# An encoder trunk on one core: two-pass partition sums, an early last norm, a ring of its own for the operand sums, constants loaded by the mix

## The chip, the cores and the metric

The kernel runs on one core of one Trainium2 chip. The core has engines that each run their own instructions strictly in order: TensorE (PE, matmuls, with the weight loads shown as PEld), VectorE (DVE), ScalarE (ACT) and GpSimd (POOL); SyncE (SP) issues most DMA transfers, GpSimd some. The metric is the device time of one execution in microseconds (us). In the names of the trace `out<-in` stands for what an instruction writes and reads, with buffer numbers left out.

## The reference

Two layers (DEPTH 2) work on x of 512 tokens by 1024 channels. Each layer is a feed-forward block, a token-mixing block of three branches, and a second feed-forward block; a last norm ends the program. Cut to what matters here:

```python
def rmsnorm(x, g):
    y = x * lax.rsqrt(jnp.mean(x * x, axis=-1, keepdims=True) + NORM_EPS)
    return y * g

def swiglu_ffn(h, w_in, w_out):            # w_in 1024 x 5632, w_out 2816 x 1024
    gate, up = jnp.split(h @ w_in, 2, axis=-1)
    return (jax.nn.silu(gate) * up) @ w_out

# in rwkv7_mixer (8 heads of 64), and in gla_mixer (4 heads of 128):
kk = kk / jnp.maximum(jnp.linalg.norm(kk, axis=-1, keepdims=True), 1e-12)
bonus = jnp.sum(r_h * k_h * r_k, axis=-1, keepdims=True) * v_h
o = o * lax.rsqrt(jnp.mean(o * o, axis=-1, keepdims=True) + NORM_EPS) * norm_w

for l in range(DEPTH):
    x = x + 0.5 * swiglu_ffn(rmsnorm(x, ffn1_norm[l]), ffn1_w_in[l], ffn1_w_out[l])
    h = rmsnorm(x, mix_norm[l])
    ...                                    # RWKV-7, gated linear attention (GLA), memory attention
    x = x + merged @ w_out[l]
    x = x + 0.5 * swiglu_ffn(rmsnorm(x, ffn2_norm[l]), ffn2_w_in[l], ffn2_w_out[l])
return rmsnorm(x, final_norm)
```

All data are float32.

## The kernel before

**Layout.** Activations lie transposed: channels on the 128 partitions, the 512 tokens along the row. x is eight tiles of 128x512. A sum over channels or over the 64 or 128 channels of a head is therefore a sum over partitions, and is made on TensorE: a matmul with a constant matrix of ones (`ones`), of ones in blocks of 64 (`blk`) or with a column of ones (`one`). These constants and some masks lie side by side in one array `cst` in memory.

**Split products.** A large product runs as three matmuls of type fp32r: each operand is split into `hi`, a rounded copy that ACT writes, and `lo`, the remainder that DVE writes by subtracting `hi`. The products are hi*hi, lo*hi and hi*lo. Plain fp32 matmuls are used where the operands are not split, among them the partition sums.

**A feed-forward block** (`ffn`, L787) goes over 11 column blocks twice (b = 0, 1), and after each eleven it multiplies by the second matrix, eight output tiles. A column block is done in one of two ways. `whole` (L800) multiplies 256 columns directly, with four weight tiles `wraw` of 128x512 (256 KB each) and 48 matmuls of 512 tokens. The other way (`loads` L815, `begin` L829, `middle` L840, `end` L850) is a scheme with seven smaller products instead of eight. It works on two halves of the tokens with sums of operands, and takes 84 matmuls of 256 tokens. It needs sums of activations, made once per block by `half_sums` (L739), and sums of weights. The weight sums are begun by the transfers themselves: `fs`, a tile of 128x2x512, is first filled from SP's queue with one 256 KB weight part written twice, and then GpSimd issues a second transfer into it that adds two other parts (`accum_op=ALU.add`). `wa` is one more part on its own. The first `NWHOLE` = 2 (L28) column blocks with b = 0 are whole, so that the sums can be made meanwhile; all others are done in the second way.

**Rings.** A tile name's tag has a fixed number of buffers. A new use waits until the oldest user's readers are through. `fs` has three buffers, and in the kernel before the tile in which `half_sums` makes its differences (`t`, L748) uses the same tag, so the four of these and the first weight sums of each feed-forward block go through one ring of three.

**The norm of a block** (`norm_in` L685, `rstd` L719): ACT squares the eight x tiles, DVE adds them up to `sqa`, four small fp32 matmuls with `one` sum over partitions into `ps_f`, ACT takes the root (`rt`, after an ACT_TABLE_LOAD), DVE the reciprocal, four fp32 matmuls with the identity (`ps_f<-cst,rt`) broadcast it, and DVE copies it to `rs`. The column blocks need `rs` only after their products. The last norm (`finish`, L1596) uses the same function after the last product and then scales the eight x tiles and stores them.

**Order.** The program is not issued as it is written. A Recorder notes every operation; a planner (`cost` L323, `choose` L385) then sets one order for each engine and for SP from estimated durations, and `issue` (L541) writes it out. It also decides when a transfer is issued; it gives a transfer a duration of its own, with no account of others in flight. All instructions are written in one helper, so every row of the trace shows line L288, and tile names tell them apart.

Of the kernel before, what the change touches and what calls it, by code (L numbers as in the profile page):

```python
# [19 lines left out]
P = 128  # L20
# [7 lines left out]
NWHOLE = 2  # L28
# [18 lines left out]
for _name, _w in (("ident", 128), ("blk", 128), ("mrwkv", 128),  # L47
                  ("eye", 64), ("in4", 64), ("up1", 128), ("up2", 128), ("lev4", 128),
                  ("lev8", 128), ("lev16", 128), ("reset", 512), ("mgla", 256), ("ones", 128)):
    CONST[_name] = (_n, _w)  # L50
    _n += _w
# [504 lines left out]
class Net:  # L556
# [14 lines left out]
    def c(self, name):  # L571
        o, w = CONST[name]
        return self.cst[:, o:o + w]
# [15 lines left out]
    def setup(self):  # L589
# [10 lines left out]
        self.cst = self.const.tile([P, NCONST - 384], F32, name="cst", tag="cst")  # L600
        for c0, c1 in ((0, P), (P, NCONST - 384)):
            nc.sync.dma_start(out=self.cst[:, c0:c1], in_=I["cst"][:, c0:c1])
# [6 lines left out]
        nc.vector.memset(self.one, 1.0)  # L609
        self.yd = self.dram.tile([3, P, T], F32, name="yd", tag="yd")  # L610
# [15 lines left out]
    def mix_params(self):  # L626
        nc, I, l = self.nc, self.I, self.l
        c = self.gp.tile([P, 384], F32, name="mgla", tag="mgla")
        nc.sync.dma_start(out=c, in_=I["cst"][:, NCONST - 384:])
        self.mgla = c[:, 0:256]  # L630
        self.ones = c[:, 256:]
# [44 lines left out]
    def split(self, hi, lo, src, scale=None):  # L676
# [4 lines left out]
        else:  # L681
            nc.scalar.activation(hi, src, AF.Copy, scale=scale)
            nc.vector.scalar_tensor_tensor(lo, src, scale, hi.bitcast(F32), ALU.mult, ALU.subtract)

# [54 lines left out]
    def half_sums(self, pool, xs, norm):  # L739
# [6 lines left out]
        for q in range(4):  # L746
            h = pool.tile([P, 4, H], F32, name="fh", tag="fq", bufs=2)
            t = pool.tile([P, 4, H], F32, name="fs", tag="fs", bufs=3)  # L748
# [38 lines left out]
    def ffn(self, w_in, w_out, norm, aside=None):  # L787


        nc = self.nc  # L790
        with ExitStack() as ctx:
# [4 lines left out]
            for b in range(2):  # L796
# [66 lines left out]
                if b == 0:  # L863
                    for j in range(NWHOLE):
# [8 lines left out]
                if aside is not None and b == 0:  # L873
                    aside(pool)
                for o in range(KD):
# [93 lines left out]
    def rwkv_gates(self, hp, hf, wz, r, k, v):  # L969
# [4 lines left out]
        if hf == 0:  # L974
# [3 lines left out]
            sq, self.nrm_k = (self.lr.tile([P, T], F32, name=n, tag="ush", bufs=2) for n in ("ksq", "knrm"))  # L978
            nc.scalar.activation(sq, self.kk, AF.Square)
            psn = self.small("i")  # L980
            nc.tensor.matmul(psn, self.c("blk"), sq, start=True, stop=True)
# [23 lines left out]
    def rwkv_first(self, hp, hf, r, k, v, kk, kh, a, G):  # L1005
# [96 lines left out]
        nc.tensor.matmul(ps, self.c("blk"), rk, start=True, stop=True)  # L1102
# [290 lines left out]
    def gla_pair(self, pool, hp, al, yh, yl, between):  # L1393
# [70 lines left out]
        for j in range(2):  # L1464
# [14 lines left out]
            nc.tensor.matmul(ps, self.ones, sq, start=True, stop=True)  # L1479
# [116 lines left out]
    def finish(self, out):  # L1596
        nc = self.nc
        rs, _ = self.rstd(self.x, T, D, self.pool("fin", 1), copy=False)
        for k in range(KD):
            nc.vector.scalar_tensor_tensor(self.x[k], self.x[k], self.pcol("final_norm", k), rs, ALU.mult, ALU.mult)  # L1600
# [79 lines left out]
```

## Time and profile before

| what | value |
|---|---|
| time, median of 3 runs | 2659.07 us (2658.54 to 2660.87) |
| the profiled execution | 2659.52 us, of which the span of instructions is 2657.5 us |
| mean granted TensorE clock | 0.996 |

The program's stretches, with PE's busy time in each and the mean busy share of the 16 DMA engines:

| stretch, us from the span's start | what | PE busy us | DMA share |
|---|---|---|---|
| 0 to 60 | start of the first feed-forward block | 50.68 of 60 | 0.84 |
| 60 to 367 | rest of it | 307.00 of 307 | 0.59 |
| 367 to 975 | mix of layer 0 | 603.77 of 608 | 0.25 |
| 975 to 1332 | second feed-forward block | 356.36 of 357 | 0.58 |
| 1332 to 1690 | first feed-forward block of layer 1 | 355.86 of 358 | 0.60 |
| 1690 to 2300 | mix of layer 1 | 606.50 of 610 | 0.26 |
| 2300 to 2640 | second feed-forward block | 337.49 of 340 | 0.56 |
| 2640 to 2657 | last norm and stores | 3.94 of 17 | 0.33 |

A row of the timeline has the start, the duration, the engine, the operation and how many of it follow each other; in brackets stands how long the engine was idle before, and what it waited for. Matmuls overlap in these rows, so their rate is read from start to start. A row of the waits has the engine's tile that waited, what released it, the idle time, the number of waits, and the longest. SPq and POOLq are the issues of transfers by these engines; a DMA row has the time from issue to landing. In a table of windows the columns are the stretch; its length and PE's busy time (and instructions); the busy time of PEld, DVE, ACT and POOL; the granted clock; the DMA share; and the rate in GB/s.

### The profile page before, as it was taken

What the parts mean: (1) busy time and instruction counts of PE and PEld (TensorE: products, weight loads), DVE (VectorE), ACT (ScalarE), POOL (GpSimd) and SP (SyncE); (2) the same over time, 40 slices, a digit from 0 to 9 for tenths busy, and PEclk for the clock granted to TensorE, in tenths of its full rate; (3) what the DMA queues carried; (4) which work ended last, traced back from release to release, by engine and by line L of the source; (5) the groups of instructions that cost most, each with busy time, mean ns of one, the idle gap of its engine ahead of it and who ended that gap; (6) DMA issues with size and microseconds to landing.
All of it is one profiled execution on the core that took longest, in us unless ns stands there. A gap on an engine that the chain in (4) does not pass through costs nothing.

```text
span 2657.5 us, 43379 instructions
## 1 busy us (share of the span) xinstructions
PE 2621.6 (99%) x16136; PEld 2299.9 (87%) x16136; DVE 1909.5 (72%) x3915; ACT 1403.3 (53%) x2727; POOL 91.9 (3%) x194
## 2 busy tenths in 40 slices
PE   8999999999999999999999999999999999999997
PEld 7989988888888889899899898878888888898996
DVE  8949666687886569678497594766888864794873
ACT  7626457465554356446465363665655543663552
POOL 0000000000000001000000000000000000010000
PEclk9999999999999999999999999999999999999998
DMA  8837342211121348565386463422212123584642
GB/s 233 205 107 181 117 147 80 103 62 62 64 66 66 108 137 203 139 153 125 108 203 159 128 159 123 152 85 83 70 58 80 60 80 100 159 201 120 170 110 79
DMA packets 127859, 321.98 MB, mean 121 GB/s; under 512 B 13312, under 2 KB 28096, under 8 KB 127648
## 3 DMA queue, kind: packets, MB, share of 16 engines
q1 hardware_dynamic: 116128, 277.26, 34.2%
q0 software_dynamic: 11520, 41.95, 8.9%
q8 instruction: 127, 2.08, 0.3%
q14 instruction: 84, 0.69, 0.1%
HBM read 307.10 MB, written 12.06 MB: 120 GB/s over the span
## 4 chain that ended last, share of the span: by engine, by line
PE 88%; DVE 7%; DMA 3%; ACT 1%; issue 1%; SPq 0%; DVEq 0%; POOL 0%; ACTq 0%; POOLq 0%
PE ps_b L288 56%; PE ps_i L288 16%; PE ps_f L288 7%; PE ps_c L288 7%; PE ps_y L288 2%; DMA fs<-in_ffn_in_dram 2%; DVE wlo L288 1%; DVE lo L288 1%; DVE t L288 0%; DMA wraw<-in_ffn_in_dram 0%; DVE sqa L288 0%; DVE x L288 0%; DVE Z L288 0%; DVE fs L288 0%; DVE knrm L288 0%
## 5 line engine op out<-in xcount | busy, mean ns | idle before, releaser
L288 ACT ACTIVATE whi<-wraw 128x512 fp32r<-128x512 f32 x522 | 320.9, 616 | 580.7 <-PE ps_b L288 527.0
L288 DVE TENSOR_TENSOR wlo<-wraw,whi 128x512 fp32r<-128x512 f32 (+1 forms) x520 | 347.7, 669 | 332.9 <-ACT whi L288 326.5
L288 PE MATMUL ps_b<-xhi,whi 128*128 128x512 f32 (+1 forms) x880 | 354.1, 403 | 0.1
L288 PE MATMUL ps_b<-xlo,whi 128*128 128x512 f32 (+1 forms) x880 | 351.8, 400 | 0.0
L288 PE MATMUL ps_b<-xhi,wlo 128*128 128x512 f32 x864 | 347.0, 402 | 0.0
L288 PE MATMUL ps_b<-mhi,wlo 128*128 128x512 f32 x704 | 277.2, 394 | 0.0
L288 PE MATMUL ps_b<-mlo,whi 128*128 128x512 f32 x704 | 275.8, 392 | 0.0
L288 PE MATMUL ps_b<-mhi,whi 128*128 128x512 f32 x704 | 273.7, 389 | 0.0
L288 PE MATMUL ps_i<-t,hi 128*128 128x256 f32 x1280 | 235.6, 282 | 0.5 <-ACT ft L288 0.5
L288 PE MATMUL ps_b<-xhi,hi 128*128 128x256 f32 (+1 forms) x704 | 206.4, 293 | 6.6 <-ACT hi L288 6.5
L288 PE MATMUL ps_b<-xlo,hi 128*128 128x256 f32 (+1 forms) x704 | 206.1, 293 | 0.3 <-DVE xlo L288 0.3
L288 PE MATMUL ps_b<-xhi,lo 128*128 128x256 f32 (+1 forms) x704 | 206.2, 293 | 0.1
L288 PEld LDWEIGHTS ps_i<-t,hi 128*128 128x128 f32 x1280 | 197.7, 190 | 0.8 <-ACT ft L288 0.7
L288 PEld LDWEIGHTS ps_b<-xlo,whi 128*128 128x128 f32 (+1 forms) x880 | 164.2, 187 | 36.1 <-issue 2.9
L288 PEld LDWEIGHTS ps_b<-xhi,whi 128*128 128x128 f32 (+1 forms) x880 | 164.4, 187 | 34.2 <-issue 2.6
L288 PEld LDWEIGHTS ps_b<-xhi,wlo 128*128 128x128 f32 x864 | 162.7, 188 | 32.1 <-issue 1.0
L288 PE MATMUL ps_i<-t,lo 128*128 128x256 f32 x640 | 180.0, 281 | 0.0
L288 PEld LDWEIGHTS ps_b<-mlo,whi 128*128 128x128 f32 x704 | 132.2, 188 | 30.3
L288 ACT ACTIVATE hi<-wraw 128x512 fp32r<-128x512 f32 x192 | 120.2, 628 | 72.3 <-PE ps_b L288 65.7
L288 PEld LDWEIGHTS ps_b<-mhi,whi 128*128 128x128 f32 x704 | 132.2, 188 | 28.9
L288 PEld LDWEIGHTS ps_b<-mhi,wlo 128*128 128x128 f32 x704 | 132.3, 188 | 26.8
L288 ACT ACTIVATE hi<-fq 128x512 fp32r<-128x512 f32 x160 | 101.0, 631 | 98.5 <-PE ps_i L288 84.1
(348 smaller groups left out, 6193.0 us busy)
## 6 DMA issues: line engine op xcount, KB each, us to landing
wraw<-in_w_main_dram SPq DMA_DIRECT2D x108, 512.0 KB, 3.3
fs<-in_ffn_in_dram SPq DMA_DIRECT2D x80, 512.0 KB, 5.7
fs<-in_ffn_in_dram POOLq DMA_DIRECT2D x80, 512.0 KB, 7.6
wraw<-in_ffn_in_dram SPq DMA_DIRECT2D x80, 512.0 KB, 4.9
wraw<-in_ffn_out_dram SPq DMA_DIRECT2D x64, 512.0 KB, 3.6
wa<-in_ffn_in_dram SPq DMA_DIRECT2D x80, 256.0 KB, 4.6
wraw<-in_ffn_out_dram SPq DMA_DIRECT2D x64, 192.0 KB, 2.3
wraw<-in_w_branch_dram SPq DMA_DIRECT2D x48, 256.0 KB, 2.6
```

Source lines behind the costliest of these rows:

```text
L288: return getattr(getattr(self.tc.nc, engine), what)(*(f(v) for v in a), **{n: f(v) for n, v in k.items()})
```

## The change

It has five parts.

1. **Partition sums in two passes.** The sums for the RWKV key norm (`ksq`, 8 matmuls of 512 tokens), the RWKV bonus (`rk`, recorded as `t`, 16 of 256) and the GLA norm (`gc`, 8 of 512) were single fp32 matmuls. A new function `total` splits the operand into `hi` (ACT) and `lo` (DVE) and makes two fp32r matmuls with an fp32r copy of the constant.
2. **The last norm's sums.** `finish` now squares and adds the x tiles as each becomes final. The eighth tile's square is not added by DVE; it goes straight into four more accumulating matmuls. A dummy root, issued earlier in the last feed-forward block, loads the table.
3. **A ring of its own.** The differences of `half_sums` get the tag `ts` with two buffers; `fs` is left to the weight sums.
4. **Whole blocks.** `NWHOLE` becomes a table: 3 in the first feed-forward block of layer 0, and 2 elsewhere.
5. **Constants.** Only the identity (64 KB) is loaded at the start. Each mix loads the other constants: a tile `mxc` of 1408 columns (704 KB), and 512 columns instead of 384 in `mgla`, where `blk` now lies beside `ones`. At the start 1536 further columns (768 KB) were loaded before.

```diff
-NWHOLE = 2
+NWHOLE = [[3, 2], [2, 2]]
...
-        self.cst = self.const.tile([P, NCONST - 384], F32, name="cst", tag="cst")
-        for c0, c1 in ((0, P), (P, NCONST - 384)):
-            nc.sync.dma_start(out=self.cst[:, c0:c1], in_=I["cst"][:, c0:c1])
+        self.cst = self.const.tile([P, P], F32, name="cst", tag="cst")
+        nc.sync.dma_start(out=self.cst, in_=I["cst"][:, :P])
...
-        c = self.gp.tile([P, 384], F32, name="mgla", tag="mgla")
-        nc.sync.dma_start(out=c, in_=I["cst"][:, NCONST - 384:])
+        self.mxc = self.mx.tile([P, NCONST - 512 - P], F32, name="mxc", tag="mxc")
+        nc.sync.dma_start(out=self.mxc, in_=I["cst"][:, P:NCONST - 512])
+        c = self.gp.tile([P, 512], F32, name="mgla", tag="mgla")
+        nc.sync.dma_start(out=c, in_=I["cst"][:, NCONST - 512:])
         self.mgla = c[:, 0:256]
-        self.ones = c[:, 256:]
+        self.sums["ones"] = self.gp.tile([P, P], F32R, name="ones_r", tag="ones_r")
+        nc.scalar.activation(self.sums["ones"], c[:, 256:384], AF.Copy)
+        self.sums["blk"] = self.mx.tile([P, P], F32R, name="blk_r", tag="blk_r")
+        nc.scalar.activation(self.sums["blk"], c[:, 384:], AF.Copy)
...
+    def total(self, ps, name, hi, lo, src):
+
+        nc = self.nc
+        nc.scalar.activation(hi, src, AF.Copy)
+        nc.vector.tensor_tensor(lo, src, hi.bitcast(F32), ALU.subtract)
+        for i, a in enumerate((hi, lo)):
+            nc.tensor.matmul(ps, self.sums[name], a, start=i == 0, stop=i == 1)
...
-            t = pool.tile([P, 4, H], F32, name="fs", tag="fs", bufs=3)
+            t = pool.tile([P, 4, H], F32, name="ts", tag="ts", bufs=2)
...
-                    for j in range(NWHOLE):
+                    for j in range(NWHOLE[l][norm == "ffn2_norm"]):
...
+                if b == 1 and last:
+
+                    self.root = self.nrm.tile([P, 4], F32, name="rt", tag="rt", bufs=2)
+                    nc.scalar.activation(self.root[:, 0:1], mhi[:, NFB - 1, 0:1].bitcast(F32), AF.Sqrt,
+                                         bias=self.eps[:, 0:1], scale=0.0)
...
-            sq, self.nrm_k = (self.lr.tile([P, T], F32, name=n, tag="ush", bufs=2) for n in ("ksq", "knrm"))
+            sq = self.lr.tile([P, T], F32, name="ksq", tag="ush", bufs=2)
             nc.scalar.activation(sq, self.kk, AF.Square)
             psn = self.small("i")
-            nc.tensor.matmul(psn, self.c("blk"), sq, start=True, stop=True)
+            hi = self.lr.tile([P, T], F32R, name="khi", tag="khi", bufs=1)
+            lo = self.lr.tile([P, T], F32R, name="klo", tag="ush", bufs=2)
+            self.total(psn, "blk", hi, lo, sq)
+            self.nrm_k = self.lr.tile([P, T], F32, name="knrm", tag="ush", bufs=2)
...
-        nc.tensor.matmul(ps, self.c("blk"), rk, start=True, stop=True)
+        hl = self.lr.tile([P, T], F32R, name="khi", tag="khi", bufs=1)
+        hi, lo = hl[:, :N], hl[:, N:]
+        self.total(ps, "blk", hi, lo, rk)
...
-            nc.tensor.matmul(ps, self.ones, sq, start=True, stop=True)
+            hi, lo = (q.tile([P, T], F32R, name=n, tag=n, bufs=1) for q, n in ((self.lr, "khi"), (pool, "glo")))
+            self.total(ps, "ones", hi, lo, sq)
...
-        rs, _ = self.rstd(self.x, T, D, self.pool("fin", 1), copy=False)
+
+        nc = self.nc
+        acc, sq = (self.keep.tile([P, T], F32, name="sqa", tag=t) for t in ("kT", "vm"))
+        rt = self.root
+        for k in range(KD - 1):
+            nc.scalar.activation(sq if k else acc, self.x[k], AF.Square)
+            if k:
+                nc.vector.tensor_tensor(acc, acc, sq, ALU.add)
+        nc.scalar.activation(sq, self.x[KD - 1], AF.Square)
+        ps = self.small()
+        for i, a in enumerate((acc, sq)):
+            for t in range(4):
+                nc.tensor.matmul(ps[:, t:t + 1], a[:, t * P:(t + 1) * P], self.one, start=i == t == 0,
+                                 stop=i == 1 and t == 3, skip_group_check=True)
+        nc.scalar.activation(rt, ps[:, 0:4], AF.Sqrt, bias=self.eps[:, 0:1], scale=1.0 / D)
+        nc.vector.reciprocal(rt, rt)
+        ps = self.small()
+        for t in range(4):
+            nc.tensor.matmul(ps[:, t * P:(t + 1) * P], rt[:, t:t + 1].to_broadcast([P, P]), self.c("ident"),
+                             start=True, stop=True)
         for k in range(KD):
-            nc.vector.scalar_tensor_tensor(self.x[k], self.x[k], self.pcol("final_norm", k), rs, ALU.mult, ALU.mult)
+            nc.vector.scalar_tensor_tensor(self.x[k], self.x[k], self.pcol("final_norm", k), ps, ALU.mult, ALU.mult)
...
-            self.ffn(self.I["ffn2_in"][l], self.I["ffn2_out"][l], "ffn2_norm")
+            self.ffn(self.I["ffn2_in"][l], self.I["ffn2_out"][l], "ffn2_norm", last=l == L - 1)
```

The rings, the constants and the sums all enter the planner, so instructions stand in another order now. Three places follow, as the two programs list them.

At the start of the program, on SP, from the load of the last x tile on. `cst` are constants, `par` layer parameters, `wraw` the weights of the whole blocks (a row of `wraw 128x512` is 256 KB), `wa` and `fs` those of the later blocks. Before:

```order
L288 DMA x_128<-in_x_dram 128x512
L288 DMA cst<-in_cst_dram 128x128
L288 DMA wraw<-in_ffn_in_dram 128x512
L288 DMA wa<-in_ffn_in_dram 128x512 x3
L288 DMA cst<-in_cst_dram 128x1536
L288 DMA par_164<-in_par_dram 128x124
L288 DMA wraw<-in_ffn_in_dram 128x512 x3
L288 DMA fs<-in_ffn_in_dram 128x2x512
L288 DMA wraw<-in_ffn_in_dram 128x512
```

and after:

```order
L288 DMA x_128<-in_x_dram 128x512
L288 DMA cst<-in_cst_dram 128x128
L288 DMA wraw<-in_ffn_in_dram 128x512
L288 DMA fs<-in_ffn_in_dram 128x2x512
L288 DMA wa<-in_ffn_in_dram 128x512
L288 DMA fs<-in_ffn_in_dram 128x2x512
L288 DMA wa<-in_ffn_in_dram 128x512
L288 DMA fs<-in_ffn_in_dram 128x2x512
L288 DMA wa<-in_ffn_in_dram 128x512
L288 DMA wraw<-in_ffn_in_dram 128x512
L288 DMA par_179<-in_par_dram 128x124
L288 DMA wraw<-in_ffn_in_dram 128x512 x7
```

The three `fs` loads now stand ahead of the fifth weight load, the first of the second whole block; the large `cst` load is gone. Before, that weight load stood behind `wa`, `cst` and `par`, and the first `fs` behind two more.

At the start of the second feed-forward block of layer 0, on SP, behind the last read of the mix (`xold`). Before:

```order
L288 DMA xold<-xd 128x512
L288 DMA wraw<-in_ffn_in_dram 128x512 x3
L288 DMA wa<-in_ffn_in_dram 128x512 x3
L288 DMA wraw<-in_ffn_in_dram 128x512 x2
L288 DMA fs<-in_ffn_in_dram 128x2x512
L288 DMA wraw<-in_ffn_in_dram 128x512
L288 DMA wraw<-in_ffn_in_dram 128x1024 x2
```

and after:

```order
L288 DMA xold<-xd 128x512
L288 DMA wraw<-in_ffn_in_dram 128x512 x3
L288 DMA fs<-in_ffn_in_dram 128x2x512
L288 DMA wa<-in_ffn_in_dram 128x512
L288 DMA fs<-in_ffn_in_dram 128x2x512
L288 DMA wa<-in_ffn_in_dram 128x512
L288 DMA fs<-in_ffn_in_dram 128x2x512
L288 DMA wraw<-in_ffn_in_dram 128x512
L288 DMA wa<-in_ffn_in_dram 128x512
L288 DMA wraw<-in_ffn_in_dram 128x512 x2
```

Three `fs` loads now stand ahead of the sixth weight load and its successors; before, one stood behind the seventh. The starts of the two later feed-forward blocks have changed in the same way, with two or three `fs` loads ahead.

At the same place, on ACT, in the program after (`hi<-wraw` is the rounding of a weight tile, `fh` and `n`, `t` belong to `half_sums`, `rt` is the root of the norm):

```order
L288 ACTIVATE sq<-x_128 128x512
L288 ACTIVATE hi<-wraw 128x512
L288 ACTIVATE fh<-x_77,par_75 128x512
L288 ACTIVATE fh<-x_113,par_75 128x512
L288 ACTIVATE n_10148<-ts 128x2x256
L288 ACTIVATE hi<-wraw 128x512
L288 ACTIVATE t_10160<-ts 128x256
L288 ACT_TABLE_LOAD
L288 ACTIVATE rt<-ps_f,eps 128x4
L288 ACTIVATE hi<-wraw 128x512
```

The two roundings ahead of the table load are those of the sixth and the seventh weight tile, so `rt` stands behind them.

More of the change, by code (lines that the diff above doesn't have):

```diff
@@ L46 @@
 _n = 0
-for _name, _w in (("ident", 128), ("blk", 128), ("mrwkv", 128),
+for _name, _w in (("ident", 128), ("mrwkv", 128),
                   ("eye", 64), ("in4", 64), ("up1", 128), ("up2", 128), ("lev4", 128),
-                  ("lev8", 128), ("lev16", 128), ("reset", 512), ("mgla", 256), ("ones", 128)):
+                  ("lev8", 128), ("lev16", 128), ("reset", 512), ("mgla", 256), ("ones", 128), ("blk", 128)):
     CONST[_name] = (_n, _w)
@@ L572, in c @@
         o, w = CONST[name]
-        return self.cst[:, o:o + w]
+        return self.cst[:, o:o + w] if o < P else self.mxc[:, o - P:o - P + w]
     def pcol(self, name, i):
@@ L609, in setup @@
         nc.vector.memset(self.one, 1.0)
+        self.sums = {}
         self.yd = self.dram.tile([3, P, T], F32, name="yd", tag="yd")
@@ L785, in part, with ffn @@
         nc.kind = 0
-    def ffn(self, w_in, w_out, norm, aside=None):
-        nc = self.nc
+    def ffn(self, w_in, w_out, norm, aside=None, last=False):
+        nc, l = self.nc, self.l
         with ExitStack() as ctx:
```

## The prediction

> **What bounds the kernel now.** I read the page's busy times first, then PE's waits, then the chain that ended last.
>
> ```profile
> PE 2621.6 (99%) x16136; PEld 2299.9 (87%) x16136; DVE 1909.5 (72%) x3915; ACT 1403.3 (53%) x2727; POOL 91.9 (3%) x194
> PE 88%; DVE 7%; DMA 3%; ACT 1%; issue 1%; SPq 0%; DVEq 0%; POOL 0%; ACTq 0%; POOLq 0%
> PE ps_f L288 <- DVE sqa L288: 8.3, 2, 6.1
> PE ps_b L288 <- ACT hi L288: 6.5, 1, 6.5
> PE ps_c L288 <- ACT hi L288: 2.3, 2, 2.1
> ```
>
> TensorE is busy for 99% and makes 88% of the chain, so the time is PE's work plus PE's few stalls. A change counts if it alters PE's passes, or if it opens or closes a stall. The large stalls are at the two ends: 6.5 us for the first weights, 6.1 us at the last norm. What DMA, ACT or DVE gain elsewhere is hidden behind PE.
>
> **Terms on PE: two-pass sums, and the third whole block.**
>
> ```profile
> L288 PE MATMUL ps_i<-ksq,cst 128*128 128x512 f32 x16 | 8.3, 599 | 0.0
> L288 PE MATMUL ps_i<-gc,mgla 128*128 128x512 f32 x16 | 8.2, 595 | 0.0
> L288 PE MATMUL ps_i<-t,cst 128*128 128x256 f32 x32 | 10.3, 404 | 0.3 <-DVE t L288 0.2
> 552.39 1.02 PE L288 MATMUL ps_i<-ksq,cst 128*128 128x512 f32 x2
> 553.25 0.59 PE L288 MATMUL ps_f<-kT,xq 128*128 128x256 f32 x2
> 738.36 0.59 PE L288 MATMUL ps_i<-t,cst 128*128 128x256 f32 x2
> 738.79 0.38 PE L288 MATMUL ps_y<-S,AR 128*128 128x128 f32 x2
> 2559.24 2.86 PE ps_i L288 x24
> 2577.69 60.46 PE ps_b L288 x264
> ```
>
> A fp32 matmul leaves two records. The three groups are therefore 8, 8 and 16 matmuls. From start to next start a fp32 one of 512 takes 0.86 us (552.39 to 553.25), one of 256 takes 0.43 (738.36 to 738.79). The split type runs 264 matmuls of 512 in 60.46 us, 0.229 each, and 24 of 256 in 2.86, 0.119 each. Removed: 16 x 0.86 + 16 x 0.43 = 20.64. Added: 32 x 0.229 + 32 x 0.119 = 11.14. Term: **-9.5 us**. The new split on ACT and DVE costs about 0.6 and 0.7 us for each of 32 sums (the square and the STT of the tail, below, are of that size). PE has other work in the mix, and in these rows it waits 0.0 and 0.3 us, so I take nothing; if the cover failed at every sum PE would lose 1.3 x 32 = 42 us, and I keep 5 us of that, some one in eight, as the upper end.
>
> The third whole block has 48 matmuls of 512 in place of 84 of 256: 48 x 0.229 - 84 x 0.119 = **+1.0**.
>
> **The end.**
>
> ```profile
> 2630.81 0.62 ACT L288 ACTIVATE sqa<-x 128x512 f32<-128x512 f32 x1
> 2638.16 0.69 DVE L288 SCALAR_TENSOR_TENSOR x<-ps_b,x 128x512 f32<-128x512 f32 x1 [6.40 <-PE ps_b L288]
> 2638.77 5.39 DVE L288 TENSOR_TENSOR sqa<-sqa,sq 128x512 f32<-128x512 f32 x7
> 2643.25 1.28 ACT L288 ACT_TABLE_LOAD   x1
> 2644.22 1.87 PE L288 MATMUL ps_f<-one,sqa 128*128 128x1 f32 x8 [6.09 <-DVE sqa L288]
> 2646.12 0.26 ACT L288 ACTIVATE rt<-ps_f,eps 128x4 f32<-128x4 f32 x1 [1.59 <-PE ps_f L288]
> ```
>
> All seven additions stand behind the last x tile: 2638.86 to 2644.22, 5.36 us before PE can sum. After the change only a square (0.62, and some 0.05 to hand over) stands there: -4.7. Four further sums now run ahead in PE's stream. Eight records took 1.87 us here at the end and 1.05 at the start, so they cost some 1.1 (at most 1.87). The table load was hidden under the additions; the early dummy root keeps it off this path. Without that cover it would put its 1.28 back. Term: **-3.6**.
>
> **The start, gains.** DVE's additions keep PE waiting 2.26 us at 23.50 (the row is below), and `ps_c` waits 2.3 us in two places for `hi`, whose weight sums share a ring with the activation sums. With a ring apart, and PE later there anyway, I count both as gone: **-2.3 and -2.3**.
>
> **The start, a new stall.** What the ring held back now stands ahead of weights on SP.
>
> ```profile
> 9.00:12.00 3.00, 2.64 (x10) 1.36 (x8) 2.46 (x4) 3.00 (x5) 0.00 (x0) 1.00 1.06 395
> 11.49 0.33 SPq L288 DMA_DIRECT2D cst<-in_cst_dram  x1
> 12.91 5.71 DMA wraw<-in_ffn_in_dram
> 16.81 0.43 SPq L288 DMA_DIRECT2D fs<-in_ffn_in_dram  x1
> wraw<-in_ffn_in_dram SPq DMA_DIRECT2D x1, 256.0 KB, 3.6
> fs<-in_ffn_in_dram SPq DMA_DIRECT2D x1, 512.0 KB, 5.5
> 18.65 0.63 ACT L288 ACTIVATE hi<-wraw 128x512 fp32r<-128x512 f32 x1 [0.70 <-DMA wraw<-in_ffn_in_dram]
> 20.61 0.39 PE L288 MATMUL ps_b<-xhi,hi 128*128 128x512 f32 x1
> 23.50 0.72 PE L288 MATMUL ps_f<-one,sqa 128*128 128x1 f32 x5 [2.26 <-DVE sqa L288]
> ```
>
> The 9 to 12 us window shows DMA share 1.06 and 395 GB/s: the engines are full. The fifth weight tile, issued at 12.91, lands at 18.62; ACT rounds it by 19.28, and PE uses it at 20.61. The slack is 1.3 us. The two rows behind the issue at 16.81 are the window around it: the weight tile just ahead lands at about 20.0 and that `fs` at 22.3, so a full queue serves one `fs` in 2.3 us. In the changed order the fifth tile loses 768 KB of `cst` (2.0 us at 395 GB/s) and 0.1 of `par`, and gains three `fs` (6.9): it lands at 18.6 - 2.1 + 6.9 = 23.4. Its rounding ends at 24.1, where PE wants it at 20.6: a stall of 3.5 us, if no other queue takes a share.
>
> Another does. Each `fs` that has landed releases GpSimd's transfer into it, and two land before the fifth tile does.
>
> ```profile
> fs<-in_ffn_in_dram POOLq DMA_DIRECT2D x1, 512.0 KB, 5.8
> 48.25 0.38 SPq L288 DMA_DIRECT2D fs<-in_ffn_in_dram  x1
> 48.47 0.86 POOL L288 DMA_DIRECT2D fs<-in_ffn_in_dram  x1 [1.60 <-DVE lo L288]
> fs<-in_ffn_in_dram SPq DMA_DIRECT2D x1, 512.0 KB, 9.2
> fs<-in_ffn_in_dram POOLq DMA_DIRECT2D x1, 512.0 KB, 9.6
> q0 software_dynamic: 288, 1.05, 42.1%
> ```
>
> The first row is such a transfer with little beside it: 5.8 us. The others are 46 to 59 us: the `fs` of 48.25 takes 9.2 us instead of 5.5 with GpSimd's transfers around it. In these 13 us GpSimd's queue moved two transfers' bytes (1.05 MB) and took 42.1% of the engines: 0.421 x 13 / 2 = 2.7 us of all engines for each. So the stall is 3.5 with none ahead of the tile, 6.2 with one, **8.9** with two. The two ends are far apart; the case of 48.25, where SP's load did pay, is the nearest row, and I take two.
>
> **The other three starts.** The second feed-forward block of layer 0 stands for them.
>
> ```profile
> 968.88 5.81 SPq L288 DMA_DIRECT2D wraw<-in_ffn_in_dram  x3
> wraw<-in_ffn_in_dram SPq DMA_DIRECT2D x1, 256.0 KB, 3.3
> 975.70 0.40 PE L288 MATMUL ps_i<-xhi,hi 128*128 128x512 f32 x1
> ```
>
> The third load of the first row, the fifth weight tile, is issued at 974.4 and lands 3.3 us later (second row), at 977.7. Three `fs` (6.9), two or three `wa` and two weight tiles (0.66 each, 256 KB at 395 GB/s) follow: the sixth tile lands at about 986.5, the seventh at 987.9. ACT rounds that tile and a piece of the activation sums and loads the root's table ahead of the norm's root, and then DVE takes the reciprocal: 0.63 + 0.4 + 1.28 + 0.26 + some 0.2 = 2.8, so PE gets the root to broadcast at 990.7. PE starts at 975.70 and has 60 passes ahead of that broadcast, 60 x 0.232 = 13.9 (a bit above 0.229, as the rows run there), and arrives at 989.6. The stall is 1.1 us with none of GpSimd's transfers ahead, 3.8 with one and 6.5 with two. Two again: **3 x 6.5 = +19.5**. What is late next is ACT's and DVE's own queue, `hi` and `lo` of later tiles behind the waiting root; PE then has those late as well, which the stall already contains.
>
> **Constants of the mix.** The window of the first mix:
>
> ```profile
> 367.00:975.00 608.00, 603.77 (x3328) 499.50 (x3327) 430.62 (x990) 322.31 (x657) 9.79 (x52) 1.00 0.25 82
> ```
>
> Each mix loads 704 KB and 64 KB more on SP, 2.0 us of a full queue, but a quarter of the DMA engines is in use there. Between 0 and 2.0 each I take 0.5: **+1.0**.
>
> **Sum.** -9.5 + 1.0 - 3.6 - 4.6 + 8.9 + 19.5 + 1.0 = +12.7. The profiled execution is 2659.5 (span 2657.5 and 2.0 around it), 0.45 above the median: 2672.2, or **2672** by the median too.
>
> **The rivals.** (A) The forecast, with both of GpSimd's transfers ahead of the weights. Its own range is 2664 to 2684: the lower end has one transfer fewer at each start (-2.7 x 4 = 10.8, with some of it kept), the upper one more.
>
> (B) The weights land in time, and the gains stand alone. Rows for it: the fifth tile has 1.3 us of slack at the start and the stall of each of the other three starts is 1.1 us at the least. Without any GpSimd transfer ahead the stalls are 3.5 + 3 x 1.1 = 6.8, and the time is 2659.5 - 16.7 + 6.8 = 2650, to which the constants add up to 1. If the three later starts hide theirs wholly it is 2646. Against it stands 48.25.
>
> (C) The change comes out even. GpSimd's transfers take only the time of their bytes: 512 KB at 395 GB/s is 1.3 us. The stalls are then 3.5 + 2.6 = 6.1 and 3 x (1.1 + 2.6) = 11.1, and the sum is -16.7 + 17.2 + 1.0 = +1.5: 2661. The Trainium skill, page "DMA: Bandwidth & Descriptors", section "Anatomy of one DMA — SWDGE (gpsimd) path", fits 2.0 us plus the bytes at 436 GB/s for a transfer of this kind, an estimate of 1.2 us of moving for 512 KB, and by it the sum would be +0.7. The trace disagrees: 5.8 us alone where the fit has 3.2, and 2.7 us of all engines each, which is why this stays a rival.
>
> (D) Slower than the forecast. The split's ACT and DVE steps come onto the chains of the mix, where PE's next work depends on the sum (key norm, bonus); the price is up to 5 us, and with one more of GpSimd's transfers at each start (10.8) about 2684. It decides from the point where a sum's reader is PE's next instruction; the 0.3 us wait in the `t` row speaks against it.
>
> That the change doesn't do what it says is in the ring's part: if PE's wait of 2.3 us at `ps_c` was not the ring's, 2.3 is not won.
>
> **How the numbers follow.** What can be told from no change is about 0.2%, 5.3 us: 2653.8 and 2664.4 are the bounds. Chances: A 0.49, B 0.23, C 0.17, D 0.11. B is faster (0.23), C within the bounds (0.17), A and D slower (0.60). The range for 8 in 10 goes from B's 2646, all gains with nothing but the first stall, to 2688, which is the sum of 2672 with 10.8 and the mix's 5. The term with the greatest doubt is the 19.5: it hangs on one case, 48.25, carried to other places.
>
> **What would show it right or wrong.** In the changed profile PE should stall at about 20 us for `hi`, released by ACT and behind it by a `wraw` transfer landing near 24 to 29. At 989, 1350 and 2320 PE should wait at `ps_f<-cst,rt` or just behind, for several us each. The sums should appear as fp32r pairs without idle time before them, and the last product's end and the span's end should be some 15 us apart, not 19. If there is no wait over 2 us at the three later starts, the main term is wrong and B holds. If the first stall is over 12 us or PE waits at the sums, D does.

## The result and the profile after

The changed kernel takes 2687.1 us (median of 4 runs, 2684.49 to 2688.68), the kernel before 2658.8 in the same comparison. The ratio is 1.0105, with a 95% interval of 1.0088 to 1.0123: slower by 28 us. The forecast was 2672, slower by 13. The time lies just inside the upper end of the range for 8 in 10 (2688) and above that of the forecast case itself (2664 to 2684), and the change is more than twice as large as forecast. The profiled execution took 2686.56 us with a span of 2684.8; the span grew by 27.3.

The page's busy times and the waits of PE in the changed kernel:

```profile
PE 2626.1 (98%) x16108; PEld 2307.4 (86%) x16108; DVE 1920.6 (72%) x3937; ACT 1413.7 (53%) x2757; POOL 91.5 (3%) x193
```
```profile
PE ps_f L288 <- DVE rt L288: 16.6, 4, 7.8
PE ps_b L288 <- ACT hi L288: 13.8, 2, 7.3
PE ps_f L288 <- ACT sqa L288: 1.5, 1, 1.5
```

PE is busy 4.5 us longer, though its work has become less, and it has new waits: 16.6 us for the root of the norms (16.0 of it at three starts of feed-forward blocks, 0.6 at the end), and 7.3 more for a rounded weight tile. The 6.1 us at the last norm have shrunk to 1.5.

The two spans are cut where the same products end: the last product of each feed-forward block and of each mix. Each row has the stretch; its length and PE's busy time (and instructions); PEld, DVE, ACT, POOL; the clock; the DMA share; GB/s. Before:

```profile
0.00:357.10 357.10, 347.78 (x2328) 319.23 (x2329) 259.03 (x490) 194.44 (x363) 18.98 (x27) 1.00 0.63 166
357.10:975.50 618.40, 614.17 (x3412) 509.75 (x3411) 439.71 (x1005) 330.10 (x671) 9.79 (x52) 1.00 0.26 85
975.50:1321.30 345.80, 345.16 (x2322) 318.66 (x2321) 252.09 (x464) 182.52 (x339) 17.27 (x20) 1.00 0.58 147
1321.30:1669.30 348.00, 345.86 (x2322) 319.82 (x2321) 251.31 (x467) 181.36 (x339) 18.62 (x23) 1.00 0.59 155
1669.30:2292.50 623.20, 619.70 (x3424) 510.35 (x3423) 450.25 (x1016) 332.55 (x676) 9.94 (x52) 1.00 0.27 86
2292.50:2637.70 345.20, 344.56 (x2321) 318.52 (x2320) 246.12 (x456) 177.61 (x332) 17.29 (x20) 1.00 0.56 144
2637.70:2657.50 19.80, 4.37 (x18) 3.56 (x16) 10.98 (x17) 4.70 (x7) 0.00 (x0) 0.59 0.29 106
```

After:

```profile
0.00:367.00 367.00, 352.87 (x2291) 321.94 (x2292) 255.91 (x481) 192.01 (x357) 18.10 (x26) 0.99 0.60 157
367.00:985.60 618.60, 611.88 (x3412) 510.67 (x3412) 448.48 (x1021) 334.37 (x687) 10.07 (x52) 1.00 0.27 86
985.60:1339.60 354.00, 346.16 (x2321) 319.80 (x2320) 253.44 (x465) 184.82 (x341) 17.26 (x20) 0.99 0.56 143
1339.60:1694.30 354.70, 348.29 (x2322) 321.06 (x2321) 250.54 (x466) 180.60 (x338) 18.61 (x23) 0.99 0.59 153
1694.30:2317.90 623.60, 615.43 (x3424) 509.99 (x3423) 454.50 (x1031) 338.42 (x694) 10.18 (x52) 1.00 0.28 88
2317.90:2670.00 352.10, 347.98 (x2329) 321.29 (x2328) 251.48 (x463) 182.60 (x338) 17.28 (x20) 0.99 0.56 140
2670.00:2684.80 14.80, 3.46 (x18) 2.65 (x16) 6.22 (x10) 0.89 (x2) 0.00 (x0) 0.62 0.38 142
```

The four feed-forward blocks are longer by 9.9, 8.2, 6.7 and 6.9 us, 31.7 together. The mixes, which were to win 8.5 us, are longer by 0.2 and 0.4. The tail is 5.0 us shorter.

At the start the stall is the one that the forecast described. The chain in the order of time, with the landing of the fifth weight tile; the shares of the two DMA queues are below it (window 15.5 to 30 us: packets, MB, share of the 16 engines):

```profile
15.53 13.32 DMA wraw<-in_ffn_in_dram
28.88 0.64 ACT hi L288
29.56 6.53 PE ps_b L288 x16
```
```profile
q0 software_dynamic: 393, 1.45, 50.6%
q1 hardware_dynamic: 1279, 2.17, 48.5%
```

The tile lands at 28.86; the forecast had 23.4 and twice 2.7, 28.8. GpSimd's queue took half of the engines: 0.506 x 14.5 us for 1.45 MB, that is 2.65 us for each transfer of 0.524 MB. What the forecast did not have is in the row of PE: 16 passes of 512 take 6.5 us, where they take 3.7 at 0.229 each. The windows around them:

```profile
25.00:30.00 5.00, 0.44 (x1) 0.44 (x2) 0.46 (x1) 1.12 (x3) 0.27 (x1) 0.50 1.01 232
30.00:35.00 5.00, 5.00 (x13) 3.80 (x13) 3.76 (x8) 3.81 (x9) 0.00 (x0) 0.50 0.36 101
35.00:40.00 5.00, 5.00 (x27) 4.27 (x26) 5.00 (x13) 4.97 (x11) 0.00 (x0) 0.98 0.40 134
```

After the idle stretch the granted clock is 0.50, until about 35 us. In the timeline a pass then takes 0.427 us from start to start (30.16 to 34.42: ten passes in 4.26).

At the three later starts PE waits at the place that the forecast named, the broadcast of the root. The last row is the load at the head of the chain of the first of them: the tile lands at 1004.75, then come the roundings, the table load and the root, and PE goes on at 1007.61.

```profile
1007.61 2.07 PE L288 MATMUL ps_f<-cst,rt 128*128 128x128 f32 x8 [7.84 <-DVE rt L288]
1359.66 2.08 PE L288 MATMUL ps_f<-cst,rt 128*128 128x128 f32 x8 [4.07 <-DVE rt L288]
2336.62 2.08 PE L288 MATMUL ps_f<-cst,rt 128*128 128x128 f32 x8 [4.12 <-DVE rt L288]
990.56 14.19 DMA wraw<-in_ffn_in_dram
```

### The profile page after: what moved, and what is told of

The parts are those of the page before. It is cut to its first block, busy times and chain, and to the rows that moved or that the text cites. A ratio compares the mean times of both kernels' runs of the same rounds, so it can differ in the third digit from the quotient of the medians.

```text
span 2684.8 us, 43432 instructions
## 1 busy us (share of the span) xinstructions
PE 2626.1 (98%) x16108; PEld 2307.4 (86%) x16108; DVE 1920.6 (72%) x3937; ACT 1413.7 (53%) x2757; POOL 91.5 (3%) x193
## 4 chain that ended last, share of the span: by engine, by line
PE 86%; DVE 7%; DMA 3%; ACT 2%; issue 1%; SPq 0%; DVEq 0%; ACTq 0%
PE ps_b L288 54%; PE ps_i L288 16%; PE ps_f L288 7%; PE ps_c L288 7%; DMA wraw<-in_ffn_in_dram 2%; PE ps_y L288 2%; DVE wlo L288 1%; DVE Z L288 0%; DMA wz<-in_wz_dram 0%; DVE x L288 0%; DVE A L288 0%; ACT whi L288 0%; DVE MA L288 0%; DVE KB L288 0%; DVE knrm L288 0%
## 5 line engine op out<-in xcount | busy, mean ns | idle before, releaser
L288 DVE TENSOR_TENSOR lo<-wraw,hi 128x512 fp32r<-128x512 f32 x194 | 133.1, 686 | 50.3 <-ACT hi L288 50.2
```

Of the source, the lines that this page charges most:

```text
L288: return getattr(getattr(self.tc.nc, engine), what)(*(f(v) for v in a), **{n: f(v) for n, v in k.items()})
```

## The experiments

There are three sets: the first four kernels below, the next four and the last three. Each set was run with the kernel before on one chip, the first set on another chip than the other two. The median of the kernel before was 2660.0 us in the first set, 2656.9 in the second and 2657.6 in the third, so ratios are compared.

### The ring undone

```diff
-            t = pool.tile([P, 4, H], F32, name="ts", tag="ts", bufs=2)
+            t = pool.tile([P, 4, H], F32, name="fs", tag="fs", bufs=3)
```

> The changed kernel with one edit undone: the differences of half_sums go through the ring of fs (three buffers) again. Theory 1 (the ring of its own lets three fs loads ahead of the weights at every start of a feed-forward block): the four starts, which in the changed kernel's profile are 9.9, 8.4, 6.6 and 6.2 us longer than before, lose these 31 us but for the 1.0 of the third whole block and some 1 us; the time is 2654 to 2660 us. Rival 1 (the third whole block, or the move of the constants, makes the starts long): the starts stay long, 2680 us or more.

Measured: 2653.5 us, ratio 0.9978 (0.9969 to 0.9987). With this one line back the changed kernel is 0.22% faster than before instead of 1.05% slower; 1.0105 less 0.9978 is 1.27%, 34 us, and the time is half a microsecond under theory 1's range. The first three feed-forward blocks in its profile:

```profile
0.00:356.10 356.10, 349.11 (x2292) 319.36 (x2293) 255.38 (x481) 191.95 (x357) 18.11 (x26) 1.00 0.61 162
974.20:1322.40 348.20, 346.18 (x2322) 319.86 (x2320) 252.69 (x465) 183.53 (x340) 17.26 (x20) 1.00 0.57 146
1322.40:1667.90 345.50, 345.15 (x2322) 318.59 (x2321) 250.62 (x466) 179.71 (x338) 18.10 (x22) 1.00 0.60 157
```

They last 356, 348 and 345.5 us, where the changed kernel has 367, 354 and 355. The third whole block and the constants are still in: rival 1 falls.

### Constants and ring alone

The kernel before with parts 3 and 5 of the change; the ring needs the room that the constants' move makes.

```diff
-        self.cst = self.const.tile([P, NCONST - 384], F32, name="cst", tag="cst")
+        self.cst = self.const.tile([P, P], F32, name="cst", tag="cst")
...
+        self.mxc = self.mx.tile([P, NCONST - 512 - P], F32, name="mxc", tag="mxc")
+        nc.sync.dma_start(out=self.mxc, in_=I["cst"][:, P:NCONST - 512])
...
-            t = pool.tile([P, 4, H], F32, name="fs", tag="fs", bufs=3)
+            t = pool.tile([P, 4, H], F32, name="ts", tag="ts", bufs=2)
```

> The kernel before with two edits, the constants loaded by the mix (this makes the room in memory) and the ring of its own for half_sums. Theory 1: the starts are as long as in the changed kernel, less the third whole block, 27 to 31 us over before in all, and with what the constants cost in the mix the time is 2685 to 2697 us. Rival 1: about 2660 to 2668 us.

Measured: 2697.6 us, ratio 1.0142 (1.0125 to 1.0159), half a microsecond above theory 1's range. PE's longest waits are those of the changed kernel:

```profile
PE ps_f L288 <- DVE rt L288: 16.2, 4, 7.2
PE ps_b L288 <- ACT hi L288: 14.6, 2, 7.5
```

Against the constants alone (1.0012, next) the ring costs 1.30%, 35 us: the same as when it is taken out of the whole change.

### Constants alone

> The kernel before with one edit: the constants are loaded by the mix (blk is copied by ACT once in each mix). Theory 2 (in the mix the late constants cost about what the two-pass sums save, so that the mixes came out 0.1 and 0.4 us longer instead of 4.2 shorter): each mix is 3 to 4 us longer, at the start nothing or up to 2 us is won, 2663 to 2667 us. Rival 2 (the constants are hidden; the splits on ACT and DVE eat the saving): within 1.5 us of before.

Measured: 2663.5 us, ratio 1.0012 (1.0003 to 1.0021). Its two mixes:

```profile
358.20:978.40 620.20, 615.24 (x3411) 510.08 (x3410) 439.78 (x1005) 330.11 (x672) 9.79 (x52) 1.00 0.27 86
1668.30:2294.30 626.00, 621.15 (x3424) 510.64 (x3423) 450.37 (x1016) 332.55 (x677) 10.45 (x53) 1.00 0.27 87
```

They are 1.8 and 2.8 us longer than before (618.40 and 623.20). That is 4.6 us for something hidden at an estimated 1.0. The whole grew by some 3 us, since the two feed-forward blocks between the mixes became 3.9 us shorter (689.9 us from 978.40 to 1668.30, against 693.8 before). The time lies in theory 2's range, and its rival (hidden constants) falls; but the mixes grew by less than the 3 to 4 us each that theory 2 gave them.

### GpSimd's transfers left out

```diff
-                    nc.gpsimd.dma_start(out=s, in_=src[:, 0:2 * T].rearrange(...), accum_op=ALU.add)
+                    if b or j not in js[:3]:
+                        nc.gpsimd.dma_start(out=s, in_=src[:, 0:2 * T].rearrange(...), accum_op=ALU.add)
```

> The changed kernel, but GpSimd's transfers into the first three fs tiles of each feed-forward block are left out, so these weight sums lack two of their three parts and the result is another. Order and all else stay. Theory 1a (GpSimd's transfers ahead of the weights take 2.7 us of SP's queue each): the first stall falls from 7.4 to about 2 us, those of the other starts from 8.0, 4.2 and 4.3 to 1 or 2, the slow clock behind them goes too, and the time is 2662 to 2670 us. Rival 1a (SP's own three fs loads are the delay): the stalls stay within 1.5 us of those of the changed kernel and the time is 2682 us or more.

Measured: 2659.8 us, ratio 1.0001 (0.9992 to 1.0010), 27 us under the changed kernel. The fifth weight tile is issued at 13.49 and takes, in the issues of that moment, the first row; the second is the same tile in the changed kernel, issued at 15.53:

```profile
wraw<-in_ffn_in_dram SPq DMA_DIRECT2D x1, 256.0 KB, 8.3
```
```profile
wraw<-in_ffn_in_dram SPq DMA_DIRECT2D x1, 256.0 KB, 13.3
```

It lands at 21.8 instead of 28.9, with SP's three `fs` still ahead of it. PE's wait for that tile falls from 7.3 to 1.6 us, and those for the root from 16.6 us in four to 6.6 in three. So GpSimd's transfers in flight are what makes the queue late; SP's own three loads, which stand in place of the constants there, make the tile 3 us later than before (21.8 against 18.6). For the time rival 1a falls, and the time is 2 us under theory 1a's range.

It does not fall at every start. The wait for the root goes from 7.8 to 2.4 us in the second block and from 4.1 to nothing in the last, but only from 4.1 to 3.6 in the first block of layer 1, where SP's own loads must be the delay, as no transfer of GpSimd's is left. What that block saves is a second wait, of 1.8 us, and slow passes: the clock does not fall in it.

The planner reckoned without the transfers too, so the order is not quite that of the changed kernel: at the start the same three `fs` and three `wa` stand ahead of the fifth tile in another order, and in the second block two `fs` instead of three stand ahead of the sixth.

### The order alone

The changed kernel with its ring, and one dependence given to the planner:

```diff
                     nc.sync.dma_start(out=s, in_=src[:, 3 * T:4 * T].unsqueeze(1).to_broadcast([P, 2, T]))
+                    if b == 0 and j in js[:3]:
+                        nc.ops[-1].deps[gate] = None      # gate: the last load of the whole blocks
```

> The changed kernel with its ring of its own kept; only the planner is told that the fs loads of the first three split-scheme blocks of each feed-forward block depend on the last weight load of its whole blocks, so SP issues them behind these. Theory 1b (the order on SP is the cause, the ring only its occasion): the stalls at the four starts go as in the kernel without the ring, 2651 to 2658 us. Rival 1b (the weight sums are then late themselves, and PE waits at the first blocks of the split scheme, since a chain of two transfers of 5 to 10 us stands behind the weights): 2665 us or more.

Measured: 2658.6 us, ratio 1.0009 (1.0000 to 1.0018), half a microsecond above theory 1b's range. The ratio falls by 0.96%, some 25 of the 28 us are gone with the ring in place, so the order on SP is the cause and the ring its occasion. In the run before, nearly the same order without GpSimd's transfers cost nothing either: the loss takes both, the early `fs` loads and what they release. What remains is a smaller piece of rival 1b, PE waiting for the rounding of a late weight sum where the split scheme begins (3.1 us in the last feed-forward block):

```profile
PE ps_f L288 <- ACT hi L288: 3.6, 2, 3.1
```

### Constants and two-pass sums

The kernel before with parts 1 and 5.

```diff
-            nc.tensor.matmul(psn, self.c("blk"), sq, start=True, stop=True)
+            self.total(psn, "blk", hi, lo, sq)            # and so for the other two kinds of sums
```

> The kernel before with two edits: the constants loaded by the mix and the partition sums in two passes. The constants alone measured 2663.5 us. Theory 2 (the sums save PE's time; the constants cost it again): 4.7 us less for each of two mixes by the forecast's sum, 2 to 3.5 by the two profiles compared so far, so 2654 to 2660 us. Rival 2 (the splits on ACT and DVE eat the saving): 2661 us or more.

Measured: 2656.6 us, ratio 0.9999 (0.9990 to 1.0009). The mixes:

```profile
358.90:975.70 616.80, 611.68 (x3411) 508.94 (x3410) 447.13 (x1021) 334.47 (x688) 10.08 (x52) 1.00 0.27 86
1665.00:2288.70 623.70, 617.20 (x3423) 509.59 (x3422) 457.26 (x1032) 338.64 (x694) 10.68 (x53) 1.00 0.27 87
```

Against the constants alone they are 3.4 and 2.3 us shorter: 5.7 us where the forecast had 9.5. PE's busy time falls by 3.6 and 4.0; its idle time (length less busy) stays at 5 us in the first mix and grows from 4.9 to 6.5 in the second. So of the 3.8 us missed about half is PE's own work and half new idle time, 1.8 us. The two profiles come from two chips, but outside the mixes their stretches agree within 0.7 us; by the ratios of the times the sums save 3.5 us (1.0012 to 0.9999), give or take as much.

Rival 2 falls, for the most of the saving is there. PE's waits for two tiles of the mix that DVE makes are longer here than with the constants alone, where the one for `y` is 0.6 us and the one for `KB` is too small to be listed (under 0.2):

```profile
PE ps_f L288 <- DVE y L288: 2.2, 3, 1.1
PE ps_i L288 <- DVE KB L288: 1.9, 5, 0.6
```

Whether the splits on DVE or the planner's other order make them longer was not separated. In the changed kernel a pair stands apart and between other passes:

```profile
570.00 0.40 PE L288 MATMUL ps_i<-khi,blk_r 128*128 128x512 f32 x1
570.24 0.39 PE L288 MATMUL ps_b<-yl,whi 128*128 128x512 f32 x1
570.70 0.40 PE L288 MATMUL ps_i<-klo,blk_r 128*128 128x512 f32 x1
```

This one costs 0.24 and 0.23 to the next start, as forecast; where PE loses the 2 us was not settled.

### The constants' place in the queue

```diff
         nc.sync.dma_start(out=self.mxc, in_=I["cst"][:, P:NCONST - 512])
+        nc.ops[-1].deps[self.gate_op] = None              # gate_op: the last weight load of the memory projections
```

This was put on the kernel without the ring, and on the one with the order repaired.

> The changed kernel with the shared ring again, and with the planner told that the load of the 1408 constant columns depends on the last weight load of the memory projections, so SP issues it behind them. The kernel without this edit measured 2653.5 us; in its profile PE waits 1.9 us at the start of the first mix, for a weight tile whose load stands behind these constants. Theory 2a (their place in SP's queue is what the constants cost): both mixes become 1 to 2.5 us shorter, 2649 to 2652 us. Rival 2a (the cost is spread over the mix): within 1 us of 2653.5.

> The changed kernel with both planner edits of this set, and with its ring of its own kept. If theories 1b and 2a both hold: 2648 to 2655 us. If either falls: 2657 us or more.

Measured: 2652.6 us, ratio 0.9980 (0.9971 to 0.9990), and 2654.3 us, ratio 0.9988 (0.9979 to 0.9998). For the kernel without the ring the time does not show theory 2a: the ratio was 0.9978 without the edit, and 2652.6 us lies in the rival's range and not in the theory's. But these two ran in different sets. The other two ran in one set, and there the time falls by 4.3 us (2658.6 to 2654.3), inside the range given for both theories. In the changed kernel, at the start of the first mix, on SP, ACT and PE:

```profile
366.99 0.38 SPq L288 DMA_DIRECT2D mxc<-in_cst_dram  x1
367.42 0.42 SPq L288 DMA_DIRECT2D wz<-in_wz_dram  x1
373.55 0.42 ACT L288 ACTIVATE wzh<-wz 128x256 fp32r<-128x256 f32 x1 [3.51 <-DMA wz<-in_wz_dram]
373.87 0.61 ACT L288 ACTIVATE whi<-wraw 128x512 fp32r<-128x512 f32 x1
374.53 0.39 PE L288 MATMUL ps_b<-yh,whi 128*128 128x256 f32 x1 [1.34 <-ACT whi L288]
```

The small load `wz` (128 KB) stands behind the 704 KB and lands 6.1 us after its issue. ACT waits 3.5 us for it, and the rounding of PE's next weights stands behind it on ACT. Those weights were issued at 366.56, ahead of the constants, and had landed by 370.0. So PE waits for their rounding, and not, as the expectation had it, for weights that are late themselves. In the kernel without the ring and with the edit, `wz` stands ahead of the constants; ACT waits 0.4 us for it, and PE not at all. The mixes of that kernel last:

```profile
357.90:972.90 615.00, 609.60 (x3412) 509.00 (x3411) 448.40 (x1021) 335.01 (x688) 10.08 (x52) 1.00 0.27 86
1666.10:2287.80 621.70, 614.26 (x3423) 509.61 (x3422) 454.41 (x1031) 339.29 (x695) 10.65 (x53) 1.00 0.27 88
```

Without it they were 618.1 and 622.9 us: 3.1 and 1.2 less, about as theory 2a has it, but the span is only 1.6 us shorter (2648.5 against 2650.1), since the feed-forward blocks gave back 2.7.

### The last norm alone

The kernel before with part 2, the new `finish` and the early root.

> The kernel before with one edit: the last norm's sums made early. The forecast's term is 3.6 us less (4.7 at the end, 1.1 back in PE's stream); the profiles compared so far give 4.2 to 4.8. So 3.5 to 5 us under before. Rival: if the 4 more sums or the early table load disturb the last product, within 2 us of before.

Measured: 2652.2 us, ratio 0.9984 (0.9975 to 0.9993): 4.3 us less, with the forecast's 3.6 inside the interval. In the changed kernel the steps at the end read:

```profile
2670.47 0.69 DVE L288 SCALAR_TENSOR_TENSOR x<-ps_b,x 128x512 f32<-128x512 f32 x1 [6.32 <-PE ps_b L288]
2671.93 1.05 PE L288 MATMUL ps_f<-one,sqa 128*128 128x1 f32 x8 [1.50 <-ACT sqa L288]
```

PE's sums start 0.8 us after the last x tile (2671.16 is its end) instead of 5.4. They take 1.05 us and not 1.87: behind 1.5 us of idle time the granted clock is still 1.00 (2672 to 2673 us), where in the kernel before, behind 6.1 us, it was 0.50 (2644 to 2645).

### A version that beats both

The change without the ring and the third whole block, and then with the constants behind the weights of the memory projections.

```diff
-NWHOLE = [[3, 2], [2, 2]]
+NWHOLE = 2
...
-            t = pool.tile([P, 4, H], F32, name="ts", tag="ts", bufs=2)
+            t = pool.tile([P, 4, H], F32, name="fs", tag="fs", bufs=3)
```

> The kernel before with the constants loaded by the mix, the two-pass sums and the early last norm, that is, the changed kernel without the ring of its own and without the third whole block. If the parts add up: 4 us under the kernel with the first two edits, which was level with before, so 3 to 5 us under before. Against the kernel that has the third whole block as well, which stood 5.8 us under before: 1 us less by the forecast's term of that block; 1 to 2 us more if the block does what its wait for operand sums suggests, which is to cover them.

> The kernel of the run before with the planner told to put the load of the 1408 columns behind the last weight of the memory projections. By theory 2a a further 2 to 4 us less, so 5 to 9 us under before, the fastest of these kernels; by its rival no difference from the run before.

Measured: 2653.1 us, ratio 0.9983 (0.9974 to 0.9992), and 2648.7 us, ratio 0.9966 (0.9954 to 0.9979). The parts add up: sums and constants level, the last norm 4 us, the constants' place another 4.4 (its two mixes are 616.1 and 621.4 us, against 617.6 and 623.8 without). These two ran in one set, so theory 2a rests on this pair and on the one with the order repaired. The last is the fastest kernel here, 8.9 us under the kernel before. Whether the third whole block helps or harms is not told apart: 0.9978 with it and 0.9983 without.

## Why the prediction was right or wrong

For the stalls the mechanism and the sign were right, and case A was the likeliest. The size was wrong: +12.7 by the sum, +27.3 by the spans, 14.6 us more. The terms that failed are these. The mixes miss 9.1 us: the load of the constants was taken as hidden (0.5 us each, where the runs show 1.8 and 2.8), and the two-pass sums saved 5.7 us instead of 9.5. The first feed-forward block misses 4.6, because a stall was priced at its length alone, without the slow passes behind it, and because of a gain put at the wrong place. The later blocks came out near in sum, by errors that cancel. By stretches, from the two tables of windows:

| stretch | forecast | measured | what the difference is |
|---|---|---|---|
| first feed-forward block, layer 0 | 8.9 - 2.3 - 2.3 + 1.0 = +5.3 | +9.9 | slow clock behind the stall; a gain put at the wrong place |
| two mixes | -9.5 + 1.0 = -8.5 | +0.6 | sums -5.7, constants +4.6, the rest not settled |
| three later feed-forward blocks | +19.5, and 1.1 for the early sums | +21.8 | near in sum, by luck: +15.0 of idle time and +6.9 of busy time, where the forecast had 19.5 and 1.1 |
| tail | -4.7 | -5.0 | right |
| sum | +12.7 | +27.3 | |

**"Constants of the mix", 0.5 us each.** The forecast looked at the mean DMA share of 0.25 and took the load as hidden. The runs show +1.8 and +2.8, and the row for it is not the share but the queue: the planner put 704 KB ahead of a small load that ACT wanted some 3 us later, and ACT's rounding of PE's next weights stood behind it. The forecast had made an argument of this kind at the starts and did not make it here, though the order was there to read. Its bound of 2.0 us each would have been nearer, and still 0.6 short in sum.

**"Term: -9.5" for the two-pass sums.** It measured -5.7. The sign held; the rates of long uniform runs were taken for single passes (whether that is the reason was not shown), and PE's busy time fell by 7.5 us, not 9.5. Another 1.8 us are new idle time, which the forecast put at nothing. The upper end of 5 us for the splits was wide enough for that.

In the changed kernel the two terms together are not -1.1 but +0.6: over both mixes PE's busy time fell by 6.6 us and its idle time grew by 7.2. The remaining 1.7 us are not settled; the planner's order of the mix is another one too.

**"The start, gains": the second -2.3.** The 2.1 us of idle time that the row of `ps_c` spoke of lie in the first feed-forward block of layer 1 (348.00 less 345.86 in the table of before; the row stands at 1356.34), not at the start. Nor was it the ring's: with the ring undone this wait and the one at 23.50 are both gone as well. In the changed kernel another wait of 1.8 us stands in the same block, besides the new stall.

**The term that was missing: the clock behind a stall.** The forecast priced a stall at its own length. At the start PE then ran twelve passes at 0.427 us instead of 0.229, another 2.4 us. Over the four feed-forward blocks PE's idle time grew by 19.8 us (32.50 after, 12.74 before, each the sum of length less busy), where the forecast had 23.8; its busy time grew by 11.9, of which the third whole block and the early sums explain 2. Most of the other 10 us are passes at a lower clock: PE's busy time in windows of half a microsecond, times the share of the clock that is missing there, adds up to 11.0 us over the four blocks, and to 1.7 in the kernel before. The forecast's own rows had it: "eight records took 1.87 us here at the end and 1.05 at the start" goes with granted clocks of 0.50 and 1.00, and was read as a spread of prices. The Trainium skill, page "TensorE: Matmul & The Clock Gate", section "Part 1: The HAM clock gate (the "warmup" mystery)", says that an idle TensorE falls to half its clock and needs some 3.4 us of sustained work to get it back, and gives 426.7 ns for a cold pass of 512; the trace agrees on the 0.427 us and shows 5.3 us (29.56 to 34.85) at the first stall, and 3.2 to 6.0 us at the three later ones.

**"8.9 with two" and "+19.5".** The landing was forecast to 0.1 us, and that is luck: without GpSimd's transfers the tile lands at 21.8, where the forecast had 23.4 for SP's loads, and these transfers add 7.1 us, where it had 5.4. The stall was 7.3, not 8.9, because PE itself came 1.5 us late: the last of its first 24 passes starts at 16.3 instead of 14.8 us, for they go at 0.427 us each until 14.7, in the kernel before only until 9.6. Why was not settled; the profile has a granted clock of 1.00 there. The choice of two of GpSimd's transfers among none, one and two was about right at the start and in the second block (7.8 us). In layer 1 the stalls were 4.1 and 4.1; the first of these is still 3.6 without any of GpSimd's transfers, so there SP's own loads, which the forecast put at 1.1, are the most of it. Leaving these transfers out took 27 us away, so case C, which priced them at their bytes' time, some 10 us in all, falls.

**Case B**, the gains alone, is nearest to the kernel without the ring (2653.5, 5.8 us faster by the ratio): its gains were smaller than the 16.7 us of the forecast, for the reasons above. **Case D** named the splits as its mechanism; the time lies where D put it, at 2684, but not by that way: with the sums 1.8 us of idle time were new in the mixes, and the rest came from the starts and the constants.

## What to carry to other kernels

A buffer that holds a transfer back can be what keeps the weights in time. Before a ring is freed, read which loads pass which in the issuing queue, at every place where it is done, and count those that a landed load releases on another queue: here three loads in place of the constants made the tile 3 us later, and the transfers that they released 7 more. A load into a quiet stretch is not free if it stands ahead of an operand that any engine on the way to TensorE wants soon; price it by its place in the queue and not by the mean share. And a stall of some microseconds on TensorE can cost more than its length: add the passes at half the clock behind it, here 3 to 6 us of them for each stall.

## What was not expected of the hardware

- The granted clock falls to 0.50 in an idle stretch of 7.3 us on PE, and PE then runs passes at 0.427 us each for 5.3 us before it is back at 0.229. It is not the load on memory: at the end of the kernel before the clock is 0.50 with a DMA share of 0.00 (2645 to 2650 us).
- The length of a wait does not decide alone whether the clock falls. In the kernel before it fell behind a wait of 2.14 us, more than a microsecond after PE had gone on:

```profile
1356.34 0.50 PE L288 MATMUL ps_c<-n,hi 128*128 128x256 f32 x2 [2.14 <-ACT hi L288]
1358.00:1359.00 1.00, 1.00 (x6) 1.00 (x6) 1.00 (x3) 0.61 (x2) 0.78 (x1) 0.50 0.78 168
```

  In the kernel with GpSimd's transfers left out it stayed at 1.00 behind a wait of 3.64 us:

```profile
1342.35 1.16 PE L288 MATMUL ps_f<-cst,rt 128*128 128x128 f32 x8 [3.64 <-DVE rt L288]
1343.00:1344.00 1.00, 1.00 (x8) 0.91 (x7) 1.00 (x3) 1.00 (x3) 0.00 (x0) 1.00 0.01 4
```

  It also stayed behind the 2.26 us at 23.50 in the kernel before, and fell behind a wait of 1.83 us in the changed kernel (1375.51). What decides was not measured.
- A GpSimd transfer that adds 0.524 MB to a tile takes 2.65 us of all 16 engines, twice the 1.3 us of its bytes at the 395 GB/s of SP's loads. Beside such transfers a 256 KB load of SP's queue took 13.3 us from issue to landing, and 8.3 without them, with the same loads of SP's own ahead of it.
